# Stores of a PEER layer on ScalarE's queue, comparisons that read a PSUM bank, and pieces of the second layer's attention in other places

## The chip, the cores and the metric

The kernel runs on one core of a Trainium2 chip. The metric is device time in microseconds (us) of one execution. Five engines take part: PE (TensorE: matmuls; PEld are its weight loads), DVE (VectorE), ACT (ScalarE), POOL (GpSimd) and SP (SyncE, which issues DMAs). A DMA is issued by an instruction of an engine's queue; what stands behind that instruction waits until it is through.

## The reference, cut to what matters

A backbone of two layers over 512 latent and 256 context tokens, D = 1024, everything in float32. Each layer has an attention part and a PEER part (product-key experts with one neuron each).

```python
for l in range(2):
    sh1, s1, g1, sh2, s2, g2 = split(silu(c) @ w_mod[l] + b_mod[l])        # context: likewise from c_ctx
    hx = rms(x) * (1 + s1) + sh1
    q, k, v, u = split(hx @ w_in[l])
    q, k = rope(rms(q) * q_gain), rope(rms(k) * k_gain)
    o_attn = softmax(q @ [k_ctx, k].T) @ [v_ctx, v]
    o_conv = silu(layer_norm(depthwise_conv31(a * sigmoid(gate))))         # u = [a, gate]
    x = x + g1 * (concat(rms(o_attn) * beta_a, rms(o_conv) * beta_c) @ w_o[l])
    x = x + g2 * peer(rms(x) * (1 + s2) + sh2)
    if l == 0: h_ctx = ...                                                # the same for the context
return rms(x) * final_g

def peer(h):                          # 8 heads, 2 x 128 keys, 16384 experts
    s = (h @ w_pq) . sub_keys         # two scores lists of 128 for each head
    top 16 of each list, top 16 of the 16 x 16 sums -> expert (128 a token), w = softmax(best)
    return sum over experts of gelu(h . u_tab[expert]) * w * v_tab[expert]
```

In layer 1 the context is needed for its keys and values alone.

## The kernel before, in words

**Attention (`attention_layer`, L227 on).** Work is written as Python generators, and `merge` (L212) takes the next piece of the stream whose clock is furthest behind; the framework's scheduler then fixes each engine's order. Streams are the projections (`project`), the convolution taps (L406), modulations (`more_mods`, `mod`) and gathers of the PEER part before. Layer 1 loads `wqkv`, `convw`, `rope` and `gains` at its head (L283 to L286). `gq` (L289) is made of `gains`, `rot` (L293, L296) of `rope` and `gq`, and `hT` (L268 to L270) is the normalised x that the first product `qkv` (L319) reads. `context_kv` (L577) makes keys and values of one block of 128 context tokens: squares, a reciprocal root on DVE, a broadcast over the partitions (`rows`, L192), then `hC`, and the products; in layer 1 it is called once in `project` and once after the merge. `mod(l, s)` makes one of the six modulation vectors from four 1 MB blocks `wm` of the weights. The output projection (L683 on) opens two PSUM tiles with the convolution's half, `products(..., (4, 5, 6, 7))`, and then adds the attention's half, which reads `qs` (L485, L486).

**PEER (`peer_layer`, L707 on).** The latent tiles `dd` (four of 128 tokens in layer 0, td = 512; three in layer 1, td = 384) are computed densely over all 16384 experts; the other tiles (`fgt`) fetch their 128 experts a token with indirect DMAs on POOL (`uv`, L896), multiplied on DVE (L900: dot products, L889: weighted sums). The dense part runs in two stages.

- *U stage.* `u_stream` (L982) takes 128 steps. A step loads 512 KB of U (`raw`, two buffers, SP), splits it into `hi` (ACT, L989) and `lo` (POOL, L990), does 24 matmuls into a PSUM bank `ups` (L994; two banks in turn), takes the Gelu on ACT (`ge`, L996) and stores it to `gd` in DRAM (L998, issued by SP; the last 8 steps keep theirs).
- *Weights.* At the same time `w_stream` (L931) makes for each token the matrix of its expert weights over the 128 x 128 grid of keys: a one-hot comparison of the two key indices with the numbers 0 to 127 (`iota`, L955 on DVE, four tokens at a time, three buffers `o12`), scaled by the weight on ACT (L960), multiplied on PE (`wps`, L961), copied by ACT into `sg` (L963) and stored to `wd`, 2 MB for each block of 32 tokens (L965, issued by SP). The routing before it has a comparison of its own, `oh` (L813), in 100 x 8 numbers a partition.
- *V stage.* `v_stream` reads `gd` and `wd` back and multiplies with V (`vr`, L1024; `vps`, L1035).

The lines that decide the stores and the comparison:

```python
V.tensor_tensor(out=oh, in0=iota..., in1=c2[:, :, tt]..., op=ALU.is_equal)            # L955
nc.sync.dma_start(wd[:, :, (i - dd[0]) * 4 + blk]..., sg...)                          # L965
raw = up.tile([P, KD, P], F32, tag="raw", name="raw", bufs=2)                         # L985
nc.sync.dma_start(raw, io["uT"][l, c])                                                # L986
ps = pdd[0].tile([P, 512], F32, tag="dd", name="ups")                                 # L991
nc.sync.dma_start(gd[c // 4, :, c % 4], ge[:, 0:td])                                  # L998
```

Of the kernel before, what the change touches and what calls it, by code (L numbers as in the profile page):

```python
# [17 lines left out]
P = 128  # L18
# [26 lines left out]
T0 = (1.0, 1.0)  # L45
T1 = (2.0, 2.0)
CY = 2.0
# [13 lines left out]
def body(ctx: ExitStack, tc: tile.TileContext, io):  # L61
# [9 lines left out]
    def small(shape, name):  # L71
        pool, tag = cur["small"]
        return pool.tile(shape, F32, tag=tag, name=name)
# [153 lines left out]
    def attention_layer(l, st, fgs, fp, mark):  # L227
# [18 lines left out]
        work = pool("awk", 2, hst)  # L246
        hT = hp.tile([P, KD, nq * P], F32, tag="hT", name="hT")
        TW = SEQ if last else GW - 2 * PAD
        parts = [] if last else [(1, CT, [hT[:, k, SEQ:] for k in range(KD)])]
# [30 lines left out]
        convw = mid.tile([P, 4, CONVK], F32, name="convw")  # L280
        gains = hp.tile([P, 2, HD], F32, name="gains")

        wqkv = [wload(io["w_qkv"][l, c], "wqkv") for c in range(3)]  # L283
        nc.sync.dma_start(convw, io["convw"][:, l])
        nc.sync.dma_start(rope, io["rope"].rearrange("(n p) c d -> p n c d", p=P))
        nc.sync.dma_start(gains, io["gains"][l].partition_broadcast(P))  # L286

# [201 lines left out]
        def more_mods():  # L489
            for m in (((0, 2), (0, 3), (0, 4), (0, 5), (1, 0), (1, 1)) if l == 0 else ((1, 2), (1, 3), (1, 4), (1, 5))):  # L490
                yield from mod(*m, ppt)

        def conv_norm(t0, n, g0):
# [29 lines left out]
            for b in range(4):  # L523
                if t0:
                    V.scalar_tensor_tensor(yT[:, b, ys], yT[:, b, ys], vecs[:, l, b, 4:5], bc, op0=ALU.mult, op1=ALU.mult)
                else:
# [7 lines left out]
                    V.tensor_tensor(out=lo[:, 0:SEQ].rearrange("p (j t) -> p j t", j=hi.shape[1]), in0=q, in1=hi.bitcast(F32), op=ALU.subtract)  # L534
                    ylo.append(lo[:, 0:SEQ])
            done.append("latent" if t0 == 0 else "context")
            yield 2.0
# [39 lines left out]
        def context_kv(i):  # L577

            x = xT[:, :, i * P:(i + 1) * P]
            A.activation(hC, x, AF.Square)  # L580
            bc = rows(rsqrt(col_sums([hC[:, k, :] for k in range(KD)], 1), 1, 1.0 / D, EPS, "n"), 1)
            V.tensor_tensor(out=hC, in0=x, in1=bc.unsqueeze(1).to_broadcast([P, KD, P]), op=ALU.mult)
            V.tensor_tensor(out=hC, in0=hC, in1=mods[l, 1][:, :, 1:2].to_broadcast([P, KD, P]), op=ALU.mult)
            V.tensor_tensor(out=hC, in0=hC, in1=mods[l, 0][:, :, 1:2].to_broadcast([P, KD, P]), op=ALU.add)
            for _ in qkv(i):
                pass

        def project():
            for i in LAT if last else CT + LAT:
                yield from qkv(i)  # L590
                if last and i == LAT[-1]:
                    context_kv(NL)
            if last:
# [11 lines left out]
        if last:  # L605
            clock["mod"] = 100.0
            del streams["conv"]
            merge({**streams, "fg": (fgs, FD), "mod": (md, 2.4)}, clock, ("p", "fg"))
            with tc.high_priority():
                context_kv(NL + 1)  # L610
        else:
            merge(streams, clock, ("p",))
# [80 lines left out]
        for hf in range(4):  # L693
            if hf == len(ws):
                ws.append(wo_split(hf, op.tile([P, KD, WC], F32R, tag="whi", name="whi"), op.tile([P, KD, WC], F32R, tag="wlo", name="wlo")))
            while len(opened) < len(ws):
                opened.append(pbig.tile([P, 2, SEQ], F32, tag="big", name="wo"))
                products(opened[-1], ws[len(opened) - 1], (4, 5, 6, 7))
            ps = opened[hf]
            products(ps, ws[hf], (0, 1, 2, 3))  # L700
# [6 lines left out]
    def peer_layer(l, fp):  # L707
# [6 lines left out]
        with ExitStack() as outer:  # L714
# [16 lines left out]
            for i in dd:  # L731
                tops[i] = (rt.tile([P, PH, 2, TOPK], F32, name=f"top{i}"), rt.tile([P, PH, 2, TOPK], U32, name=f"tix{i}"))

            def best16(tiles, h, qT, keys, tmp):
# [50 lines left out]
            def route(i, rw, h0, h1):  # L785
# [25 lines left out]
                for h in range(h0, h1):  # L811
                    oh = rw.tile([P, TOPK, NCAND], F32, tag="oh", name="oh")
                    V.tensor_tensor(out=oh, in0=posf[:, h].unsqueeze(2).to_broadcast([P, TOPK, NCAND]),  # L813
                                    in1=iota[:, 0:NCAND].unsqueeze(1).to_broadcast([P, TOPK, NCAND]), op=ALU.is_equal)
                    (V if i == fgt[0] else G).tensor_tensor(out=oh, in0=oh, in1=cid[:, h].unsqueeze(1).to_broadcast([P, TOPK, NCAND]), op=ALU.mult)
# [115 lines left out]
            def w_stream():  # L931

                for i in dd:
# [16 lines left out]
                    for blk in range(4):  # L950
                        sg = rw.tile([P, PK // 2, 32, 2], F32, tag="sg", name="sg", bufs=2)
                        for t0 in range(0, 32, 4):
                            tt = slice(blk * 32 + t0, blk * 32 + t0 + 4)
                            oh = rw.tile([P, 2, 4, PK], F32, tag="o12", name="o12", bufs=3)
                            V.tensor_tensor(out=oh, in0=iota.unsqueeze(1).unsqueeze(1).to_broadcast([P, 2, 4, PK]), in1=c2[:, :, tt].to_broadcast([P, 2, 4, PK]), op=ALU.is_equal)  # L955
                            o1, o2 = oh[:, 0], oh[:, 1]
# [7 lines left out]
                            yield 1.9  # L964
                        nc.sync.dma_start(wd[:, :, (i - dd[0]) * 4 + blk].rearrange("g p h t e -> p g (h t e)"), sg.rearrange("p (g h) t e -> p g (h t e)", h=2))  # L965

# [15 lines left out]
            def u_stream():  # L982

                for c in range(PK):
# [5 lines left out]
                    mark.append(G.tensor_tensor(out=lo, in0=raw, in1=hi.bitcast(F32), op=ALU.subtract))  # L990
                    ps = pdd[0].tile([P, 512], F32, tag="dd", name="ups")  # L991
                    for n, (a, b) in enumerate(((hi, hhi), (hi, hlo), (lo, hhi))):
# [4 lines left out]
                    if c < PK - 8:  # L997
                        nc.sync.dma_start(gd[c // 4, :, c % 4], ge[:, 0:td])  # L998
                    else:
# [189 lines left out]
```

## Time and profile before

| | |
|---|---|
| three runs | 4172.8, 4183.14, 4179.64 us; median 4179.64 |
| the profiled execution | 4177.53 us, its span 4175.8 us |
| mean granted clock of PE | 0.953 of full speed |
| busy over the span | PE 90%, DVE 74%, ACT 43%, POOL 53% |
| attention of layer 0 | 0 to about 512 us |
| U stage of layer 0 | 512 to 1555 us |
| V stage of layer 0 | 1555 to 2316 us |
| attention of layer 1 | 2316 to 2738 us |
| U stage of layer 1 | 2738 to 3550 us |
| V stage of layer 1 and the end | 3550 to 4176 us |

A time in a row is counted from the start of the span. "[5.95 <-ACT hi L989]" behind an instruction says how long its engine had stood still before it, and which work ended last of what it waited for. An issue instruction of a DMA isn't counted as busy time.

### The profile page before, as it was taken

How to read it: one execution, taken by the hardware profiler on the slowest of the kernel's cores; microseconds unless marked ns; L12 is line 12 of the kernel's file. 1: busy time of each engine (PE TensorE's matmuls, PEld its weight loads, DVE VectorE, ACT ScalarE, POOL GpSimd, SP SyncE). 2: the span in 40 equal slices, each digit the busy share in tenths (PEclk: the TensorE clock that was granted, in tenths of full speed). 3: DMA queues.
4: the chain of work that ended last, by engine and by line, in shares of the span. 5: the costliest groups of instructions: out<-in, count | busy, mean ns of one | idle time of the engine just before them, and what ended most of it. 6: DMA issues, size and time to landing. Idle time of an engine off the chain costs nothing. (4 is left out here: it accounts for less than half of the span.)

```text
span 4175.8 us, 54192 instructions
## 1 busy us (share of the span) xinstructions
PE 3769.0 (90%) x19278; PEld 3204.7 (77%) x19278; DVE 3098.4 (74%) x5680; ACT 1811.6 (43%) x3679; POOL 2216.7 (53%) x1223
## 2 busy tenths in 40 slices
PE   8879998989988999999999779889888989898998
PEld 6547776867777777888777547679888888898897
DVE  5693369999986647898887784389877453787885
ACT  3345233336675633333333246333466564333333
POOL 0580135666665456555556356135756555665664
PEclk9989999999999999999999889899999999999999
DMA  4142135987888888988887714046676878898884
GB/s 169 58 182 81 51 119 204 331 304 244 285 285 287 268 319 338 344 322 335 339 335 292 275 41 172 21 136 241 231 247 220 259 262 283 320 345 297 315 319 140
DMA packets 327631, 1003.72 MB, mean 240 GB/s; under 512 B 24384, under 2 KB 159808, under 8 KB 264256
## 3 DMA queue, kind: packets, MB, share of 16 engines
q1 hardware_dynamic: 266128, 580.25, 40.5%
q0 software_dynamic: 59904, 419.46, 27.1%
q8 instruction: 152, 2.49, 0.2%
q14 instruction: 119, 0.97, 0.1%
q10 hardware_dynamic: 1328, 0.55, 0.0%
HBM read 884.29 MB, written 115.87 MB: 240 GB/s over the span
## 5 line engine op out<-in xcount | busy, mean ns | idle before, releaser
L990 POOL TENSOR_TENSOR lo<-raw,hi 128x1024 fp32r<-128x1024 f32 x256 | 647.1, 2529 | 572.0 <-ACT hi L989 504.7
L1028 POOL TENSOR_TENSOR vlo<-vr,vhi 128x1024 fp32r<-128x1024 f32 x256 | 629.5, 2466 | 471.4 <-ACT vhi L1027 457.4
L1035 PE MATMUL vps<-ahi,vhi 128*128 128x512 f32 (+1 forms) x2048 | 759.7, 372 | 44.5 <-DVE xT L1038 26.5
L1035 PE MATMUL vps<-alo,vhi 128*128 128x512 f32 (+1 forms) x2048 | 757.4, 370 | 3.1 <-DVE alo L974 3.1
L1035 PE MATMUL vps<-ahi,vlo 128*128 128x512 f32 (+1 forms) x2048 | 740.2, 371 | 9.2 <-POOL vlo L1028 9.1
L900 DVE SCALAR_TENSOR_TENSOR uv<-uv,hp 128x1024 f32<-128x1024 f32 x363 | 439.7, 1211 | 212.2 <-DMA uv<-in_uv,uix 212.1
L994 PE MATMUL ups<-hhi,hi 128*128 128x512 f32 (+1 forms) x2048 | 504.9, 386 | 72.2 <-ACT ge L996 34.7
L889 DVE SCALAR_TENSOR_TENSOR yp<-uv,act,yp 128x1024 f32<-128x1024 f32 x359 | 460.4, 1283 | 144.9 <-ACT act L902 144.0
L896 POOL DMA_INDIRECT uv<-in_uv,uix x384 | 447.8, 1166 | 222.0 <-DVE y L889 45.4
L994 PEld LDWEIGHTS ups<-hhi,hi 128*128 128x128 f32 x2048 | 383.7, 198 | 127.6 <-ACT ge L996 41.3
L994 PE MATMUL ups<-hhi,lo 128*128 128x512 f32 (+1 forms) x2048 | 479.0, 371 | 1.8 <-POOL lo L990 1.8
L994 PE MATMUL ups<-hlo,hi 128*128 128x512 f32 (+1 forms) x2048 | 475.1, 370 | 0.0
L1035 PEld LDWEIGHTS vps<-ahi,vhi 128*128 128x128 f32 x2048 | 391.3, 191 | 99.8 <-DVE xT L1038 30.6
L1035 PEld LDWEIGHTS vps<-ahi,vlo 128*128 128x128 f32 x2048 | 389.7, 191 | 63.2 <-POOL vlo L1028 16.2
L1035 PEld LDWEIGHTS vps<-alo,vhi 128*128 128x128 f32 x2048 | 391.6, 191 | 51.4 <-DVE alo L974 4.4
L901 ACT ACTIVATE act<-dots 128x1 f32<-128x1 f32 x384 | 77.4, 202 | 803.5 <-DVE uv L900 802.5
L994 PEld LDWEIGHTS ups<-hlo,hi 128*128 128x128 f32 x2048 | 378.8, 192 | 40.5
L994 PEld LDWEIGHTS ups<-hhi,lo 128*128 128x128 f32 x2048 | 373.4, 191 | 40.6 <-POOL lo L990 2.4
L955 DVE TENSOR_TENSOR o<-iota,xf 128x1024 f32<-128x1024 f32 x224 | 385.9, 1749 | 21.0 <-ACT o L960 9.3
L410 POOL TENSOR_TENSOR yT<-yT,tp 128x512 f32<-128x512 f32 (+1 forms) x150 | 261.4, 1743 | 211.9 <-ACT tp L409 201.7
L989 ACT CAST hi<-raw 128x1024 fp32r<-128x1024 f32 x256 | 267.0, 1043 | 217.8 <-DMA raw<-in_uT 185.3
L960 ACT ACTIVATE o<-o,wT 128x128 f32<-128x128 f32 x896 | 285.1, 392 | 152.2 <-DVE o L955 150.7
(281 smaller groups left out, 6055.0 us busy)
## 6 DMA issues: line engine op xcount, KB each, us to landing
raw<-in_uT SPq DMA_DIRECT2D x256, 512.0 KB, 4.9
vr<-in_vq SPq DMA_DIRECT2D x256, 512.0 KB, 6.0
wd<-sg SPq DMA_DIRECT2D x28, 2048.0 KB, 13.5
wm<-in_w_mod SPq DMA_DIRECT2D x48, 1024.0 KB, 6.5
w<-wd SPq DMA_DIRECT2D x32, 1024.0 KB, 6.6
gd<-ge SPq DMA_DIRECT2D x120, 256.0 KB, 6.2
ge<-gd SPq DMA_DIRECT2D x60, 512.0 KB, 7.1
w<-wd SPq DMA_DIRECT2D x32, 768.0 KB, 6.2
```

The source lines that it names most:

```text
L410: G.tensor_tensor(out=y, in0=y, in1=tp, op=ALU.add)
L889: V.scalar_tensor_tensor(y, t[:, 1, :], act[:, e:e + 1], y, op0=ALU.mult, op1=ALU.add)
L896: got = G.indirect_dma_start(out=t.rearrange("p c d -> p (c d)"), out_offset=None, in_=io["uv"], in_offset=bass.IndirectOffsetOnAxis(ap=ui ...
L900: V.scalar_tensor_tensor(t[:, 0, :], t[:, 0, :], 1.0, at["h"], op0=ALU.mult, op1=ALU.mult, accum_out=dots[:, ec])
L901: A.activation(act[:, ec], dots[:, ec], AF.Gelu)
L955: V.tensor_tensor(out=oh, in0=iota.unsqueeze(1).unsqueeze(1).to_broadcast([P, 2, 4, PK]), in1=c2[:, :, tt].to_broadcast([P, 2, 4, PK]), op ...
L960: A.activation(o2[:, j, :], o2[:, j, :], AF.Copy, scale=wT[:, t:t + 1])
L989: A.copy(hi, raw)
L990: mark.append(G.tensor_tensor(out=lo, in0=raw, in1=hi.bitcast(F32), op=ALU.subtract))
L994: PE.matmul(ps[:, 0:td], a[:, k, :], b[:, k, :], start=k == 0 and n == 0, stop=k == KD - 1 and n == 2)
L1028: mark.append(G.tensor_tensor(out=vlo, in0=raw, in1=vhi.bitcast(F32), op=ALU.subtract))
L1035: PE.matmul(ps[:, 0:td], a[:, c % 4, d * P:(d + 1) * P], b, start=c == 0 and n == 0, stop=c == 7 and n == 2)
```

## The change

1. The stores of `wd` and `gd` are issued by ACT (`nc.scalar`) in place of SP, in both layers.
2. In layer 1, where td + 128 = 512, a copy of `iota` is put into columns 384 to 511 of one of the two `ups` banks; both banks are then fixed tiles (`dds`), used in turn by even and odd steps, and both comparisons (L955, L813; now L982, L840) read the copy.
3. `gains` gets its place in a pool of the whole kernel, and its load stands at the start of `attention_layer`; the load of `rope` stands ahead of `wqkv` in the code.
4. `mod(1, 5)` leaves layer 1's modulation stream and stands in the output projection, between the opening products and those that read `qs`.
5. `context_kv` is a generator with pauses; its second call is a stream `k` of its own that starts when the gathers and the first call are done.
6. In layer 1 `conv_norm` pauses after each block; a pace of layer 0's taps goes from 2.0 to 2.6.

```diff
-T1 = (2.0, 2.0)
+T1 = (2.6, 2.0)
...
+        gains = sm.tile([P, 2, HD], F32, tag="dg", name="gains")
+        nc.sync.dma_start(gains, io["gains"][l].partition_broadcast(P))
...
-        gains = hp.tile([P, 2, HD], F32, name="gains")
+        nc.sync.dma_start(rope, io["rope"].rearrange("(n p) c d -> p n c d", p=P))
         wqkv = [wload(io["w_qkv"][l, c], "wqkv") for c in range(3)]
         nc.sync.dma_start(convw, io["convw"][:, l])
-        nc.sync.dma_start(rope, io["rope"].rearrange("(n p) c d -> p n c d", p=P))
-        nc.sync.dma_start(gains, io["gains"][l].partition_broadcast(P))
...
-            for m in (((0, 2), (0, 3), (0, 4), (0, 5), (1, 0), (1, 1)) if l == 0 else ((1, 2), (1, 3), (1, 4), (1, 5))):
+            for m in (((0, 2), (0, 3), (0, 4), (0, 5), (1, 0), (1, 1)) if l == 0 else ((1, 2), (1, 3), (1, 4))):
...
+                    if last:
+                        yield 4.5
...
-            bc = rows(rsqrt(col_sums([hC[:, k, :] for k in range(KD)], 1), 1, 1.0 / D, EPS, "n"), 1)
+            ps = small([P, P], "cs4")
+            spread(ps, [(ones[:, 0:32], hC[:, k, :]) for k in range(KD)], P)
+            yield 3.0
+            r = rsqrt(fold(ps, 1), 1, 1.0 / D, EPS, "n")
+            yield 8.0
+            bc = rows(r, 1)
...
-            for _ in qkv(i):
-                pass
+            yield 5.0
+            yield from qkv(i)
+            done.append(i)
...
-                    context_kv(NL)
+                    yield from context_kv(NL)
...
-            merge({**streams, "fg": (fgs, FD), "mod": (md, 2.4)}, clock, ("p", "fg"))
-            with tc.high_priority():
-                context_kv(NL + 1)
+            def gathered():
+                yield from fgs
+                done.append("fg")
+            def late_context():
+                while not {"fg", NL}.issubset(done):
+                    yield 1.0
+                yield from context_kv(NL + 1)
+            merge({**streams, "fg": (gathered(), FD), "mod": (md, 2.4), "k": (late_context(), 1.0)}, clock, ("p", "k"))
...
+            if last and not hf:
+                for _ in mod(1, 5, ppt):
+                    pass
             ps = opened[hf]
...
+            dds, num = [], iota
+            if td + PK <= 512:
+                dds = [pdd[0].tile([P, 512], F32, tag=f"dd{j}", name="ups", bufs=1) for j in range(2)]
+                num = dds[0][:, td:td + PK]
+                V.tensor_copy(num, iota)
...
-                                    in1=iota[:, 0:NCAND].unsqueeze(1).to_broadcast([P, TOPK, NCAND]), op=ALU.is_equal)
+                                    in1=num[:, 0:NCAND].unsqueeze(1).to_broadcast([P, TOPK, NCAND]), op=ALU.is_equal)
...
-                            V.tensor_tensor(out=oh, in0=iota.unsqueeze(1).unsqueeze(1).to_broadcast([P, 2, 4, PK]), in1=c2[:, :, tt].to_broadcast([P, 2, 4, PK]), op=ALU.is_equal)
+                            V.tensor_tensor(out=oh, in0=num.unsqueeze(1).unsqueeze(1).to_broadcast([P, 2, 4, PK]), in1=c2[:, :, tt].to_broadcast([P, 2, 4, PK]), op=ALU.is_equal)
...
-                        nc.sync.dma_start(wd[:, :, (i - dd[0]) * 4 + blk].rearrange("g p h t e -> p g (h t e)"), sg.rearrange("p (g h) t e -> p g (h t e)", h=2))
+                        nc.scalar.dma_start(wd[:, :, (i - dd[0]) * 4 + blk].rearrange("g p h t e -> p g (h t e)"), sg.rearrange("p (g h) t e -> p g (h t e)", h=2))
...
-                    ps = pdd[0].tile([P, 512], F32, tag="dd", name="ups")
+                    ps = dds[c % 2] if dds else pdd[0].tile([P, 512], F32, tag="dd", name="ups")
...
-                        nc.sync.dma_start(gd[c // 4, :, c % 4], ge[:, 0:td])
+                        nc.scalar.dma_start(gd[c // 4, :, c % 4], ge[:, 0:td])
```

What the built programs issue, at the places of the prediction (line numbers of the changed kernel are larger by 2 to 27). SP before, around the last `wd` store of layer 1:

```order
L986 DMA raw<-in_uT 128x1024
L998 DMA gd_20098<-ge 128x384
L965 DMA wd_20099<-sg 128x32x128
L986 DMA raw<-in_uT 128x1024
L998 DMA gd_20098<-ge 128x384
```

ACT of the changed kernel, around one `wd` store of layer 1 (L990 is the copy into `sg`, L1016 the cast to `hi`, L1023 the Gelu, L928 and L929 belong to the gathers):

```order
L1016 CAST hi<-raw 128x1024
L990 COPY sg<-wps 128x4x64x2
L1023 ACTIVATE ge<-ups 128x384 x2
L992 DMA wd_20099<-sg 128x32x128
L1025 DMA gd_20098<-ge 128x384 x2
L928 ACTIVATE act<-dots 128x1
L929 ACTIVATE act<-act,wk 128x1
L1016 CAST hi<-raw 128x1024
```

The next store stands directly behind `wd`, now on ACT, with a cast of `hi` behind both; on SP the loads of `raw` follow each other with no store between.

DVE of the changed kernel in layer 1's U stage, with what each instruction waits for (Activation is ACT, DMASW the gathers' DMAs):

```order
L982 TENSOR_TENSOR o_22474<-ups,xf 128x1024 [waits DVE_49,Activation_49]
L982 TENSOR_TENSOR o_22486<-ups,xf 128x1024 [waits DVE_49,PE_49]
L982 TENSOR_TENSOR o_22539<-ups,xf 128x1024 [waits DVE_49,PE_49]
L927 SCALAR_TENSOR_TENSOR uv,dots<-uv,hp 128x1024 [waits DMASW1_49]
L916 SCALAR_TENSOR_TENSOR yp<-uv,act,yp 128x1024 [waits DVE_49,Activation_49]
L982 TENSOR_TENSOR o_22584<-ups,xf 128x1024 [waits DVE_49,Activation_49]
```

And PE of the changed kernel there, at an even step, an odd one and the next even one:

```order
L1021 MATMUL ups<-hhi,hi 128x384 [waits DVE_49]
...
L1021 MATMUL ups<-hhi,hi 128x384 [waits Activation_49]
L1021 MATMUL ups<-hhi,hi 128x384 x7
L1021 MATMUL ups<-hlo,hi 128x384 x8
L1021 MATMUL ups<-hhi,lo 128x384 [waits Pool_49]
L1021 MATMUL ups<-hhi,lo 128x384 x7
L988 MATMUL wps<-o_23886 128x128 [waits PE_49,Activation_49]
L988 MATMUL wps<-o_23886 128x128 [waits Activation_49] x2
L1021 MATMUL ups<-hhi,hi 128x384 [waits DVE_49]
```

The first comparison of a group waits for ACT, by the program for the Gelu of the even step, and 48 of the even steps begin with a wait for DVE; before, no step's first matmul had that wait.

DVE at the head of layer 1, before:

```order
L196 TENSOR_TENSOR dg<-ident,rs_y 128x512
L289 TENSOR_SCALAR gq<-gains 128x64
L290 COPY gq<-gains 128x64
L268 TENSOR_TENSOR hT<-xT,rbc 128x8x128
L204 TENSOR_TENSOR hT<-xT,rbc 128x384 x8
L293 TENSOR_TENSOR rot<-rope,gq 128x4x64
L296 TENSOR_TENSOR rot<-rope,gq 128x4x32 x2
```

and changed:

```order
L289 TENSOR_SCALAR gq<-gains 128x64
...
L196 TENSOR_TENSOR dg<-ident,rs_y 128x512
L293 TENSOR_TENSOR rot<-rope,gq 128x4x64
L296 TENSOR_TENSOR rot<-rope,gq 128x4x32 x2
L270 TENSOR_TENSOR hT<-xT,rbc 128x8x128
L204 TENSOR_TENSOR hT<-xT,rbc 128x384 x8
```

`gq` moved ahead of the reciprocal root, and `rot` ahead of `hT`; SP loads `rope` behind `wqkv` and `convw` as before.

## Rows read from the trace of the kernel before

**Rows 1.** Busy time by stage: us, then PE, PEld, DVE, ACT, POOL, clock, DMA, GB/s.

```profile
512.00:1555.00 1043.00, 946.78 (x4490) 779.93 (x4490) 864.10 (x2025) 529.03 (x1240) 582.76 (x316) 0.96 0.78 262
...
2316.00:2738.00 422.00, 337.86 (x1768) 239.90 (x1766) 245.80 (x466) 178.37 (x300) 172.62 (x116) 0.88 0.32 116
2738.00:3550.00 812.00, 723.55 (x4222) 705.83 (x4223) 581.99 (x1323) 418.19 (x949) 472.17 (x238) 0.95 0.72 239
```

**Rows 2.** The chain that ended last, 2740 to 3550 us, shares by line.

```profile
by line: PE ups L994 20.3%; DMA raw<-in_uT 15.6%; DMA uv<-in_uv,uix 8.6%; DVE o L955 5.7%; PE wps L961 5.1%; issue 4.2%; DVE oh L813 3.5%; POOL lo L990 3.4%; DVE uv L900 3.2%; DVE yp L889 3.1%; DVE eid L816 2.3%; DVE tix L746 1.8%; DVE sc L
```

**Rows 3.** Waits of PE, 2738 to 3550: total us, times, longest.

```profile
PE wps L961 <- ACT sg L963: 31.0, 14, 5.6
```

**Rows 4.** The page's groups: count, busy us, mean ns, idle before.

```profile
L989 ACT CAST hi<-raw 128x1024 fp32r<-128x1024 f32 x256 | 267.0, 1043 | 217.8 <-DMA raw<-in_uT 185.3
```

**Rows 5.** Timeline around one wd store (start, duration us): SP, ACT, PE.

```profile
3278.24 0.37 SPq L965 DMA_DIRECT2D wd<-sg  x1
3278.72 8.58 SPq L986 DMA_DIRECT2D raw<-in_uT  x1
...
3292.39 1.04 ACT L989 CAST hi<-raw 128x1024 fp32r<-128x1024 f32 x1 [7.97 <-DMA raw<-in_uT]
...
3293.48 2.93 PE L994 MATMUL ups<-hhi,hi 128*128 128x384 f32 x8 [5.95 <-ACT hi L989]
```

**Rows 6.** Line 986: duration of the issue, ns min/median/max.

```profile
L986 SPq DMA_DIRECT2D raw<-in_uT x256: 327/333/11621, 508.5 to 3539.0; - x128
```

**Rows 7.** Timeline: first and last held issue, first and last PE gap.

```profile
985.79 5.04 SPq L998 DMA_DIRECT2D gd<-ge  x1
...
3460.82 8.11 SPq L986 DMA_DIRECT2D raw<-in_uT  x1
...
998.26 0.67 PE L961 MATMUL wps<-o 128*128 128x128 f32 x3 [1.37 <-ACT o L960]
...
3474.41 1.97 PE L994 MATMUL ups<-hhi,hi 128*128 128x384 f32 x5 [5.38 <-ACT hi L989]
```

**Rows 8.** The page's DMA queues: packets, MB, share of 16 engines.

```profile
q10 hardware_dynamic: 1328, 0.55, 0.0%
```

**Rows 9.** Timeline at layer 1's head: SP, DVE, PE; last the landings.

```profile
2318.53 0.44 SPq L285 DMA_DIRECT2D rope<-in_rope  x1
...
2338.70 0.20 DVE L289 TENSOR_SCALAR gq<-gains 128x64 f32<-128x64 f32 x1 [13.30 <-DMA gains<-in_gains]
...
2347.75 4.63 PE L319 MATMUL qkv<-wqkv,hT 128*128 128x256 f32 x13 [18.73 <-DVE rs_y L148]
...
rope<-in_rope SPq DMA_DIRECT2D x2, 256.0 KB, 12.1
```

**Rows 10.** Timeline of PE in layer 1's attention.

```profile
2463.66 0.80 PE L197 MATMUL rows<-dg,ones 128*128 128x128 f32 x2 [8.59 <-DVE dg L196]
```

**Rows 11.** PE at the output projection, and the modulations' busy time, 2316 to 2738.

```profile
2689.85 8.47 PE L689 MATMUL wo<-qs,w 128*128 128x512 f32 x24 [5.99 <-DVE qs L486]
...
2316.00:2738.00 422.00, 21.45 (x256) 8.52 (x256) 4.68 (x8) 0.88 0.32 116
```

**Rows 12.** Lines 955 and 900: ns min/median/max; then the mean in layer 1.

```profile
L955 DVE TENSOR_TENSOR o<-iota,xf x96: 1209/1221/5220, 3004.9 to 3444.5; 128x1024 f32<-128x1024 f32 x96
...
L900 DVE SCALAR_TENSOR_TENSOR uv<-uv,hp x363: 1187/1210/1225, 684.0 to 4091.8; 128x1024 f32<-128x1024 f32 x182
...
L955 DVE TENSOR_TENSOR o<-iota,xf 128x1024 f32<-128x1024 f32 x96 | 166.0, 1761 | 14.3 <-ACT o L960 8.0 <-PE wps L961 4.8 <-ACT ge L996 1.4
```

**Rows 13.** Layer 1's U stage: one step, one wps, the Gelu, DVE's longest wait.

```profile
3235.83 4.17 PE ups L994 x24
...
3273.77 1.05 PE L961 MATMUL wps<-o 128*128 128x128 f32 x8
...
L996 ACT ACTIVATE ge<-ups 128x384 f32<-128x384 f32 x127 | 61.1, 481 | 31.6 <-DMA gd<-ge 19.1 <-PE ups L994 12.5
...
DVE uv L900 <- DMA uv<-in_uv,uix: 131.0, 33, 10.3
```

## The prediction

> **What bounds the kernel now.** I began with the table of the stages that the change touches [rows 1]. TensorE (PE) is the busiest engine in each, so the change can only pay where PE stands still: 96 us in the dense U stage of layer 0 (1043 - 947), 84 us in the attention of layer 1 at a clock of 0.88, and 88 us in the dense U stage of layer 1. The chain of waits over the last [rows 2] is not PE alone: the load of raw has 15.6% of it (127 us of 810), the one-hot comparison L955 5.7% and L813 3.5%. PE's waits there [rows 3] give the next link: the largest ends on ACT, at the copy sg. ACT's own wait stands behind it: hi waits 185.3 us for raw over both layers [rows 4].
>
> Why raw is late is seen at one store of wd [rows 5]. SP issues wd at 3278.24; its next instruction, the issue of raw, then takes 8.58 us instead of 0.33, until 3287.30. Raw lands 13.59 us after 3278.72, ACT casts at 3292.39, and PE resumes at 3293.48 after 5.95 us of nothing. The median of a raw issue is 0.33 us and the maximum 11.6 [rows 6]. 27 of the 28 wd stores are followed by such a hold of the next gd or raw issue, the first 5.04 and the last 8.11 us [rows 7], 160.6 us together.
>
> **The profiled execution** took 4177.53 us, 2.1 below the median of 4179.64; the sum is made against 4177.5.
>
> **wd and gd go from SP to ACT's queue.** What it can give: the 26 PE gaps over 0.7 us that end 3 to 20 us after a wd store, from 1.37 us before 998 to 5.38 us before 3474 [rows 7], add up to 25 us in layer 0 and 44 us in layer 1, so 69 us is the upper end. SP's holds don't vanish, since the changed order puts a gd directly behind wd on ACT: if ACT is held there to the moment SP was, hi starts at 3287.3 instead of 3292.4, because raw has landed meanwhile, and 4 to 5 of the 5.95 us are won. If in the other extreme each hold stops PE in full, 160.6 us come in place of the 69, a loss of 92. I take a gain of 30, under half of the upper end: by the built order ACT casts hi more than a step ahead, and a step of 24 matmuls covers 4.17 us [rows 13] of a hold of 6 on average. Against it stand 268 issues on ACT, taken at the 0.33 us of raw and the 0.37 of wd [rows 5, 6]: 88 us of ACT's time. ACT is busy 51% of both U stages [rows 1], and PE waits there for it; with a tenth of that exposed (bounds 0 and 88) it is +8. Net: **-22**.
>
> Beside the queue that carries SP's loads the trace lists a second hardware queue with 0.55 MB [rows 8], which fits the three small issues that ACT has before (512, 20 and 4 KB). Whether a hold on one also holds the other, no row shows. The Trainium skill (DMA: Bandwidth & Descriptors, Issuing engines are not separate DMA queues) says that issuing from several engines saves only sequencer time, usually a small part of the transfer. Here that time itself is large, a hold of 8.58 us before a landing of about 5. By the page's rule alone the term would be 0 or a few us.
>
> **gains leaves the head of layer 1.** Before, DVE waits 13.30 us for gains, and PE 18.73 us behind it [rows 9]. Now gains lies there already, but the changed order puts the rot products that read rope ahead of hT. Rope was issued at 2318.53, ahead of gains; the landing known of it, that of layer 0, took 12.1 us. So it lands between 2330.6 and the 2338.7 at which DVE went on: 0 to 8 us are won, and the rot products are only moved. I take **-4**.
>
> **context_kv in pieces.** PE waits 8.59 us for dg, whose reciprocal root stands between convolution taps on DVE [rows 10]. Now the second block comes late, in a stream of its own, and its chain is split. Its work isn't less and taps go on beside it: 0 to 8.6 us, and I take **-6**, nearer to the upper end because the wait is that of the chain that is split. The pause in conv_norm and the new pace of layer 0 move only order; in layer 0 DVE's order before the U stage is the same, so nothing is taken for them.
>
> **mod(1,5) goes into the output projection.** PE waits 5.99 us there for qs, and the four modulations of layer 1 cost PE 21.45 us, one 5.4 [rows 11]. Placed in the gap it saves that at most; if its weights come late or qs is no longer late, 0. I take **-4**.
>
> **The comparisons read PSUM.** L955 has a median of 1221 ns, a maximum of 5220 and, in layer 1, a mean of 1761: 96 x 0.54 = 52 us of stretching. DVE's L900, of the same size and with an operand in PSUM, never leaves 1187 to 1225 in 363 instructions [rows 12]. So I expect about 1.22 us each, and the like of L813. Only what is on the chain pays: 46 us of L955 and 28 of L813 [rows 2], of which the stretched share of 30% (0.54 of 1.76) is 22; with the next delay close behind I take **-12** (0 to -22).
>
> **The bank becomes shared.** The built order shows what it costs: a group of L982 waits for the Gelu of the even step, and the next even step's first matmul waits for DVE, 48 times. Per pair PE has 2 x 4.17 us and three wps groups of 1.05 [rows 13], 11.5 in all; the new cycle is an even step of 4.17, a Gelu of 0.48 [rows 13], three comparisons of 1.22 and one or two gather products of 1.21: 9.5 to 10.7. It just fits. It doesn't where a gather product waits for its rows in between. DVE waits for uv 131 us in 33 pieces there [rows 13], 4 us each. I take **+8**; bounds 0 and, with 20 of those pieces exposed, +80.
>
> **Sum:** -22 - 4 - 6 - 4 - 12 + 8 = -40, so 4177.5 - 40 = **4137.5 us**.
>
> **The rivals.**
>
> *ACT is held and PE with it (slower).* One place: the gd behind wd on ACT, in the 16 + 12 blocks. For it: PE waits on ACT [rows 3], and a held ACT does no cast, no Gelu and no scaling, where a held SP stopped only the next load. Against: ACT's 49% of idle time. The point where it decides: the other terms give -18 and the issues +8, so -10, and the removed gaps 69; above 79 us of exposed holds, half of the 160.6, the kernel is slower. With 110 exposed it is 4177.5 - 10 - 69 + 110 = 4208.5.
>
> *The bank ties DVE to PE (slower).* With the upper bound of 80 in place of 8: -40 + 72 = +32, so 4209.5. It decides from 40 us of exposed gather waits above the 8 on. For it: DVE is busy 72% of that stage [rows 1] and waits for gathers; against: the cycle of 9.5 to 10.7 fits under 11.5.
>
> *The stores hold SP from ACT's queue too.* Then raw is as late as before, the 30 us fall away, and the sum is 4167.5; with some holds on ACT as well up to 4180. For it: a gd was held just like raw [rows 7], so the hold follows from wd and not from the held transfer. Against it: the second queue [rows 8]. By the Trainium skill (Perfetto Trace Analysis, DMA Instruction, on hardware-generated descriptors) the generator is shared and locked for one instruction at a time, and a profile's issue time includes the wait for that lock; by it this case is the expected one. No run here shows it yet.
>
> *More than I count.* If nearly all of the 69 us go and the stretching as well, -69 + 8 - 8 - 8.6 - 5.4 - 22 + 8 = -97: about 4080.
>
> **How the numbers follow.** The forecast has 0.48, the common generator 0.16, held ACT 0.16, the bank 0.10, more than counted 0.10. The range should hold eight in ten: from 4085, nearly the large gain, to 4205, just under the two slow cases. A measurement can tell about 0.3% (12.5 us) from no change. Faster: nearly all of the forecast (0.44), the large gain and a quarter of the common generator, 0.58. Same: most of that rival, a little of the forecast and of held ACT, 0.18. Slower: the slow cases, 0.24. If it is faster, I expect 4085 to 4165.
>
> **What would show it.** Right: raw issues of 0.33 us throughout; ACT hi waiting under 100 us for raw instead of 185; held gd issues of 4 to 8 us on ACT, with PE gaps after them under 2 us; L982 with mean near 1.22 us; the U stages together 30 to 50 us shorter; PE's gap at the head of layer 1 some 14 us. Wrong: PE gaps of 5 us behind wd on ACT (held ACT), raw still held (common generator), or PE waiting for DVE at even steps for more than 30 us (the bank).

## The result, and the profile after

The changed kernel takes 4296.37 us (median of four runs), the kernel before 4181.39 beside it: a ratio of 1.0282, 95% interval 1.0259 to 1.0305. It is 115 us slower, where the prediction said 40 us faster. The time lies above the range, 4085 to 4205 us.

The spans of the profiled executions are 4294.3 and 4175.8 us. Cut at PE's first instruction of each kind (first ups, first wps, first and last vps of layer 0, first qkv, ups, wps and vps of layer 1), both traces give:

```
stage (us)                              before   after   difference
attention, layer 0                       525.9   547.9     +22.0
U stage, layer 0, ahead of the weights   425.5   424.3      -1.2
U stage, layer 0, with the weights       631.4   656.1     +24.7
V stage, layer 0                         733.1   731.1      -2.0
head of layer 1 (last vps to first qkv)   31.8    31.7      -0.1
attention, layer 1                       391.4   380.1     -11.3
U stage, layer 1, ahead of the weights   268.3   257.5     -10.8
U stage, layer 1, with the weights       554.2   669.7    +115.5
V stage, layer 1, and the end            614.1   595.9     -18.2
```

The two parts of layer 1's U stage belong together, since the weights begin after fewer steps than before (ahead of them PE runs 1090 matmuls in place of 1356): 822.5 us before, 927.2 after, +105. The busy times of that stage, before and after (columns as in [rows 1]):

```profile
2739.00:3562.00 823.00, 727.98 (x4239) 709.93 (x4240) 588.81 (x1331) 421.19 (x958) 474.05 (x240) 0.95 0.72 240
```

```profile
2771.00:3698.00 927.00, 747.38 (x4238) 718.93 (x4238) 516.00 (x1331) 428.31 (x957) 433.38 (x239) 0.93 0.63 212
```

The work is the same (the counts agree). DVE is busy 73 us less, as the faster comparisons should give. But PE idles 180 us instead of 95, and at a granted clock of 0.93 in place of 0.95 the same matmuls take 19 us more. The waits of PE and DVE there, after (total us, times, longest):

```profile
PE ups L1021 <- ACT ge L1023: 56.9, 45, 2.8
PE ups L1021 <- DVE oh L840: 53.9, 12, 16.8
PE wps L988 <- ACT o L987: 31.9, 8, 6.5
...
PE ups L1021 <- DVE o L982: 4.7, 2, 4.3
...
PE wps L988 <- ACT sg L990: 1.5, 2, 1.3
...
DVE uv L927 <- DMA uv<-in_uv,uix: 172.4, 46, 11.4
DVE o L982 <- ACT ge L1023: 71.2, 21, 7.2
...
DVE eid L843 <- POOL oh L842: 48.9, 14, 7.4
...
DVE oh L840 <- ACT ge L1023: 20.1, 8, 5.1
```

Before, PE's largest wait in this stage was the copy sg [rows 3], now 1.5 us; it waited 16.2 us for Gelus and for no comparison. Now it waits 56.9 us for Gelus and 58.6 us for comparisons, 53.9 of it for the routing comparison L840 in only 12 pieces. DVE's largest wait is still the one for the gathered rows, 172.4 us where it was 131.8; its 91 us for Gelus (71.2 + 20.1) are new, 1.4 us before. The longest PE wait for a comparison, on the timelines of PE, ACT and DVE (start, duration):

```profile
2948.83 1.55 PE L1021 MATMUL ups<-hhi,lo 128*128 128x384 f32 x8
2967.15 2.29 PE L1021 MATMUL ups<-hhi,hi 128*128 128x384 f32 x6 [16.77 <-DVE oh L840]
...
2945.38 0.49 ACT L1023 ACTIVATE ge<-ups 128x384 f32<-128x384 f32 x1 [1.46 <-DMA gd<-ge]
...
2958.50 0.97 DVE L840 TENSOR_TENSOR oh<-posf,ups 128x800 f32<-128x800 f32 x1
...
2966.13 0.97 DVE L840 TENSOR_TENSOR oh<-posf,ups 128x800 f32<-128x800 f32 x1
```

The bank's Gelu was through at 2945.9, and the bank free for the next even step. But in the program's order two routing comparisons come first, and DVE reaches the first only after some 85 small routing instructions and two gather products, the second after some 35 more and two more products. The second ends at 2967.10, and 0.05 us later PE goes on. Before, PE did not depend on that chain until the weights needed it.

The stores went as intended on SP's side. The issue of raw, whose maximum was 11.6 us [rows 6], and ACT's first held issue after:

```profile
L1013 SPq DMA_DIRECT2D raw<-in_uT x256: 327/328/469, 530.2 to 3676.9; - x128
...
1005.60 0.39 ACTq L992 DMA_DIRECT2D wd<-sg  x1
1006.03 9.65 ACTq L1025 DMA_DIRECT2D gd<-ge  x1
```

Raw is never held again. 20 raw issues fall into stretches in which ACT's queue is held, and each takes 0.33 us: a hold on ACT's queue does not reach SP's. ACT's hi waits 50.3 us for raw in the whole execution, where it waited 185.3 [rows 4]. But the hold came along with wd. Of gd and raw issues over 1.5 us the trace before has 30 on SP, 165.8 us in sum; the one after 26 on ACT, 156.8 us. No cast, scaling or copy starts on ACT later than 1.3 us into a hold. In layer 0's U stage with the weights, 24.7 us longer, PE waits for just these pieces, the copy sg and the scaling o:

```profile
PE wps L988 <- ACT sg L990: 32.2, 14, 6.2
PE wps L988 <- ACT o L987: 27.4, 16, 7.4
```

Before, the two were 19.7 and 17.7 us there. The PE gaps over 0.7 us within 20 us after a wd store sum to 47.8 us in layer 0, where they were 25.4.

The one-hot comparison lost its stretching (columns as in [rows 12]), and the stage is longer all the same:

```profile
L982 DVE TENSOR_TENSOR o<-ups,xf x96: 1198/1215/1227, 3027.0 to 3594.5; 128x1024 f32<-128x1024 f32 x96
```

At the head of layer 1, gains is there early, and rope has taken its place (timeline of DVE and PE, to be read beside [rows 9]):

```profile
2382.09 0.43 DVE L293 TENSOR_TENSOR rot<-rope,gq 128x256 f32<-128x256 f32 x1 [12.77 <-DMA rope<-in_rope]
...
2391.11 1.22 PE L319 MATMUL qkv<-wqkv,hT 128*128 128x256 f32 x2 [18.17 <-DVE rs_y L149]
```

### The profile page after: what moved, and what is told of

Read it like the earlier page. It is cut to its first block, busy times and chain, and to the rows that moved or that the text cites. A ratio compares the mean times of both kernels' runs of the same rounds, so it can differ in the third digit from the quotient of the medians.

```text
span 4294.3 us, 54046 instructions
## 1 busy us (share of the span) xinstructions
PE 3794.1 (88%) x19278; PEld 3213.0 (75%) x19278; DVE 2994.1 (70%) x5681; ACT 1808.9 (42%) x3672; POOL 2177.9 (51%) x1223
## 4 chain that ended last, share of the span: by engine, by line
PE 38%; DVE 10%; DMA 9%; issue 4%; ACT 3%; POOL 3%; ACTq 2%; SPq 0%; POOLq 0%; DVEq 0%
PE vps L1062 22%; PE ups L1021 8%; DMA uv<-in_uv,uix 4%; PE wps L988 2%; ACTq L1025 1%; DMA raw<-in_uT 1%; DMA vr<-in_vq 1%; DVE alo L1001 1%; POOL vlo L1055 1%; DVE ge L997 1%; DVE uv L927 1%; ACT ge L1023 1%; PE po L460 1%; PE wo L705 1%; DVE yT L406 1%
## 5 line engine op out<-in xcount | busy, mean ns | idle before, releaser
L1017 POOL TENSOR_TENSOR lo<-raw,hi 128x1024 fp32r<-128x1024 f32 x256 | 631.6, 2468 | 768.8 <-ACT hi L1016 550.9
L1021 PE MATMUL ups<-hhi,hi 128*128 128x512 f32 (+1 forms) x2048 | 518.2, 393 | 170.5 <-ACT ge L1023 68.2
L923 POOL DMA_INDIRECT uv<-in_uv,uix x384 | 429.3, 1118 | 211.6 <-DVE y L916 42.7
L928 ACT ACTIVATE act<-dots 128x1 f32<-128x1 f32 x384 | 77.3, 201 | 811.8 <-DVE uv L927 781.9
L1016 ACT CAST hi<-raw 128x1024 fp32r<-128x1024 f32 x256 | 266.7, 1042 | 237.8 <-PE ups L1021 163.6
L988 PE MATMUL wps<-o 128*128 128x128 f32 x1792 | 259.0, 289 | 93.4 <-ACT o L987 59.4
```

Source lines behind the costliest of these rows:

```text
L923: got = G.indirect_dma_start(out=t.rearrange("p c d -> p (c d)"), out_offset=None, in_=io["uv"], in_offset=bass.IndirectOffsetOnAxis(ap=ui ...
L928: A.activation(act[:, ec], dots[:, ec], AF.Gelu)
L988: PE.matmul(ps[:, j, :], o1[:, j, :], o2[:, j, :], start=True, stop=True)
L1016: A.copy(hi, raw)
L1021: PE.matmul(ps[:, 0:td], a[:, k, :], b[:, k, :], start=k == 0 and n == 0, stop=k == KD - 1 and n == 2)
```

## The experiments

The theory after the result: the shared bank makes layer 1's U stage longer, and the stores and T1 account for layer 0. Its rival: ACT, held behind wd, does it in both layers. In the table "U1" is layer 1's U stage from the first ups to the first vps, "U0w" layer 0's U stage with the weights, "att0" and "att1" the attentions, "V1" layer 1's V stage with the end; profiled executions, us. The same stage of the same order differs by up to 9 us from one profile to another, and a profile isn't always of a typical execution: that of best is its slowest of 12 (4196.23 us), those of stores_only and T1_only are their fastest of 6.

```
run             att0    U0w    head   att1    U1      V1     ratio to before (95%)
before          525.9   631.4  31.8   391.4   822.5   614.1  1
after           547.9   656.1  31.7   380.1   927.2   595.9  1.0282 (1.0259 to 1.0305)
stores_only     527.6   636.8  32.1   393.7   819.6   622.9  1.0052 (1.0026 to 1.0077)
stores_back     544.4   623.0  31.6   379.8   929.8   607.5  1.0246 (1.0210 to 1.0281)
attention_only  548.7   626.4  31.8   382.6   818.5   613.4  1.0012 (0.9996 to 1.0028)
T1_only         550.5   633.7  32.0   387.6   817.5   617.5  1.0076 (1.0052 to 1.0100)
fixed_banks     546.5   623.2  31.7   386.7   827.0   621.8  one run, 4198.80 us
half_bank       545.2   625.3  31.6   380.2   904.5   609.0  one run, 4258.54 us
eq_only         547.4   627.4  31.8   381.3   873.3   591.7  one run, 4220.59 us
oh_only         539.4   639.0  31.4   383.7   883.5   623.1  1.0144 (1.0117 to 1.0171)
rot_late        532.7   641.6  19.6   381.9   886.0   620.0  1.0123 (1.0094 to 1.0152)
best            541.0   636.6  19.6   387.6   825.6   627.0  0.9983 (0.9971 to 0.9995)
split_only      533.4   617.1  32.1   389.8   808.2   618.1  0.9941 (0.9919 to 0.9963)
best_split      532.2   621.2  19.6   384.7   801.9   623.6  0.9915 (0.9894 to 0.9936)
```

**stores_only**: the kernel before, with both stores on ACT.

```diff
-                        nc.sync.dma_start(wd[...
+                        nc.scalar.dma_start(wd[...
-                        nc.sync.dma_start(gd[...
+                        nc.scalar.dma_start(gd[...
```

> Only the two stores are moved to ACT; the bank, the attention and T1 are those of before. Theory bank (the shared PSUM bank makes layer 1's weight stage 114 us longer, the stores cost about 24 us in layer 0 and 10 to 20 in layer 1): 4215 to 4225 us, ratio 1.008 to 1.011, layer 1's weight stage at most 20 us longer. Rival stores (ACT, held at the store behind wd, makes that loss too): 4285 to 4300 us, ratio about 1.027, layer 1's weight stage 90 to 114 us longer.

Measured: 4204.95 us, layer 1's weight stage 549.9 against 554.2. The rival falls. The stores cost 0.5%, a little less than the theory's 0.8 to 1.1%; no one stage of the profile holds that loss. Why they gain nothing is in the trace: hi waits 100.0 us for raw in place of 185.3, but the holds moved as they were (26 on ACT, 141.0 us), and the PE gaps over 0.7 us within 20 us after a wd store changed from 25.4 to 37.0 us in layer 0 and from 42.8 to 27.8 in layer 1: 68 before, 65 now. One such hold on ACT, and the raw issues:

```profile
3254.88 0.47 ACT L996 ACTIVATE ge<-ups 128x384 f32<-128x384 f32 x1
3255.39 6.28 ACTq L998 DMA_DIRECT2D gd<-ge  x1
...
L986 SPq DMA_DIRECT2D raw<-in_uT x256: 327/328/727, 510.5 to 3544.1; - x128
```

**stores_back**: the changed kernel with the stores on SP.

> The changed kernel with both stores issued by SP again; the bank, the attention and T1 stay changed. Theory bank: layer 1's weight stage stays 80 to 100 us longer than before, the time is 4250 to 4265 us, ratio 1.017 to 1.021. Rival stores: the stage is as short as before and the time 4185 to 4200 us, ratio 1.001 to 1.005.

Measured: 4279.42 us, U1 929.8. The loss in layer 1 stays in full without the stores, and was not smaller but larger than I expected of the bank: the weight stage is 117.5 us longer where I said 80 to 100, and the total is above the 4250 to 4265. Against this run the changed kernel, which differs in the stores alone, has 33 us more in U0w and about the same U1.

**attention_only**: the same without the bank.

```diff
-            if td + PK <= 512:
+            if False:
```

> The changed kernel with the stores back on SP and without the bank: what is left is T1, gains and rope, mod(1,5), context_kv and conv_norm. Both theories: layer 0's attention 22 us longer, layer 1's 11 us shorter, the U stages as before, so 4188 to 4196 us, ratio about 1.002 to 1.004. If these edits also shift the dense stages, the time would be over 4210.

Measured: 4186.6 us, a little under the expected time, the stages as expected. With stores_back it isolates the bank: 929.8 - 818.5 = 111 us of U1, but 92.8 us of the whole (4279.42 - 4186.6), since V1 is 6 us shorter with the bank and other stages differ by a few us. By the medians the changes so far add up: nothing that can be told from 0 for the attention edits with T1, 93 us for the bank, 17 for the stores beside them (4296.37 - 4279.42, from two comparisons whose intervals overlap), 111 of the 115 us.

**T1_only**: the kernel before with `T1 = (2.6, 2.0)`.

> The kernel before with the one pace T1 of layer 0 at 2.6. Theory pace (the later taps and not gains or rope make layer 0's attention longer): 4200 to 4206 us, ratio 1.004 to 1.006. Rival (the early load of gains delays x, and the rest follows): as before, 4178 to 4184 us, ratio 0.999 to 1.001.

Measured: 4211.55 us, ratio 1.0076, more than expected; layer 0's attention 550.5. So the pace does lengthen it. About half of the 24.6 us is one chain at the end of the convolution, and not the taps: DVE's first 453 instructions are the same as before, to about 395 us, all 61 taps among them. The reciprocal root of the last layer norm, at 394.9 us before, among the attention's products, comes at 441.4. The norm behind it moves along with it, to where PE has nothing else to do: PE stands 11.8 us, until 480.7. PE's waits between 300 and 552 us for such a chain, before and in T1_only:

```profile
PE rows L197 <- DVE dg L196: 6.1, 2, 5.3
...
PE rows L197 <- DVE dg L196: 18.0, 3, 11.8
```

The wait is 17.9 or 18.0 us in each of the seven profiles with 2.6, and 6.1 or 6.2 in each of the seven with 2.0. Over all profiles the attention of layer 0 takes 544 to 551 us in the seven with 2.6 and 526 to 541 in the seven with 2.0, 14 us apart on average. In the runs that also have the other attention edits part of it comes back in U0w (623 to 627 against 637 to 642), so what T1 costs the whole is settled only for this run alone.

**fixed_banks**: as stores_back, but both comparisons read `iota`.

```diff
-                                    in1=num[:, 0:NCAND]...
+                                    in1=iota[:, 0:NCAND]...
-                            V.tensor_tensor(out=oh, in0=num...
+                            V.tensor_tensor(out=oh, in0=iota...
```

> As stores_back, with the two fixed ups banks, but both comparisons read iota in SBUF again; the copy stays unread. Theory sharing (the reading of a bank that PE fills is what costs): layer 1's weight stage falls from 672 back to 545 to 560 us, total 4180 to 4195. Rival rotation (fixed tiles in place of the pool's rotation cost it): the stage stays above 650 us, total about 4280.

Measured: U1 827.0, its weight stage 556.8; the total, of one run, is 4 us above the expected 4180 to 4195. It is the reading, not the fixed pair of banks. By the reading is meant all that follows from it in the program: the built order changes with it too (ahead of the first weights PE runs 1356 matmuls here as before, 1090 in every run whose one-hot comparisons read the bank, 1134 where the routing alone does). No run has that order without the readers.

**half_bank**: L982 reads the bank in two of four blocks.

```diff
+                            ... in0=(num if blk < 2 else iota)...
```

> As stores_back, but of the four blocks of 32 tokens of each tile only the first two read the PSUM copy in L982, the last two read iota in SBUF; the routing comparison reads PSUM. Theory sharing: half of the 117 us go, the weight stage of layer 1 takes 600 to 625 us and the steps of the last two blocks are as short as before (about 6.3 us a step), those of the first two about 8. Rival (the loss comes from the order of the whole stage, which the scheduler sets around the bank): the stage is above 645 us or below 575.

Measured: the weight stage 649.5, above the 600 to 625 of the theory and, by its number, where the rival put it (above 645); U1 904.5. Half of L982's readers give back 25 us of the 103 between stores_back and fixed_banks. Either the order of the whole stage counts or the other reader does, the routing comparison; this run can't tell which.

**oh_only**: T1 at 2.0, stores on SP; only the routing comparison L840 reads the bank.

```diff
-T1 = (2.6, 2.0)
+T1 = (2.0, 2.0)
-                            V.tensor_tensor(out=oh, in0=num...
+                            V.tensor_tensor(out=oh, in0=iota...
```

> Stores on SP, T1 back at 2.0, all other attention edits kept; only the routing comparison L840 reads the PSUM copy, the one-hot comparison L982 reads iota in SBUF. Expected by the stages so far: layer 0's attention as before, layer 1's attention 9 to 12 us shorter, the part of layer 1's U stage ahead of the weights about 10 us shorter, the weight stage as before: 4155 to 4168 us, ratio 0.994 to 0.997. Rival (any reader of the shared bank delays the U steps): the weight stage over 580 us and the total over 4190.

Measured: 4250.81 us, ratio 1.0144. My expectation failed and its rival held: 32 reading instructions make U1 61 us longer than before. PE's largest wait of that stage is for them:

```profile
PE ups L1021 <- DVE oh L840: 50.3, 10, 17.3
```

**eq_only**: as stores_back; only L982 reads the bank.

> As stores_back (T1 2.6, stores on SP), but only the 96 one-hot comparisons L982 read the PSUM copy; the 32 routing comparisons L840 read iota in SBUF. Theory two readers: each of the two readers of the bank costs by itself; layer 1's U stage from its first step to the first V product takes about 870 us against 822 before, 930 with both and 884 with the routing alone, and PE waits for L840 nowhere. Rival (the routing comparison alone costs, the one-hot comparisons ride on it): 822 to 835 us.

Measured: U1 873.3 us, the 870 expected; PE waits for L840 nowhere. Against fixed_banks (827.0) the 96 one-hot comparisons cost 46 us of U1; the 32 routing comparisons cost 58 to 60 (oh_only or rot_late less best, below; rot_late differs from best in that reading alone). Together 104 to 106, and stores_back has 103 (929.8 - 827.0): about 0.5 us for each one-hot comparison and 1.8 for each in the routing. The 46 are not spread evenly: PE waits once there, for 18.3 us, for the routing's sum eid, which it does for 1.2 us in the changed kernel. And they are not all lost: V1 is 30 us shorter here than in fixed_banks, and the spans differ by 22 us only (4218.8 and 4197.0, one run each). The routing's 60 stay: rot_late's V1 is 7 us below best's, and its median is 58 us above.

**rot_late**: as oh_only, with `rot` ordered behind `hT` in layer 1.

```diff
+            if last:
+                for m in made:          # the rot products of this qk
+                    tc.add_manual_dep(m.ins, first.ins.name, ..., reason="late")   # first: the last hT of the first block
```

> As oh_only, and in layer 1 the four rot products, which read rope, are ordered behind hT. Theory head (hT waited only for whatever small load stood ahead of it on DVE, first gains, then rope): the 31.8 us from the last V product to the first qkv product fall to 18 to 23, the total is 8 to 13 us below oh_only, 4143 to 4160, ratio 0.991 to 0.995. Rival (wqkv itself is late, or the wait turns up at the next user of rot): the head or the attention behind it keeps its length and the total is that of oh_only within 4 us.

Measured: the head falls from 31.4 to 19.6 us, the median by 12.0, as the theory said of the difference; the time itself, 4238.82, is not the 4143 to 4160, which started from oh_only as I had expected it. The intervals of the two ratios overlap; the head shows it clearly. hT had only ever waited for what stood ahead of it in DVE's order.

**best**: rot_late without the bank.

> T1 at 2.0, stores on SP, no reader of the shared bank, the attention edits and rot behind hT: the parts of the change that shortened a stage, and the mended head. Expected: layer 0's attention 526 to 533 us, the head 19.6 in place of 31.8, layer 1's attention 382 in place of 391, the U and V stages as before: 4158 to 4168 us, ratio 0.993 to 0.997. Rival (layer 0's attention is longer by the early gains and not by T1): 4170 to 4180.

Measured: 4180.52 us, ratio 0.9983, barely faster than before: my expectation failed, and the time lies at the upper end of the rival's. The head (-12) and layer 1's attention (-4) are there; layer 0's attention was 541.0 in that profile, longer than the 526 to 533 expected. The four profiles with T1 at 2.0 and the other attention edits have 532 to 541, the three without those edits 526 to 533, so something beside T1 may lengthen it too; 7 us on average, within what one profile differs from another, settle nothing.

**best_split**: as best, and each wd store in two halves on two queues.

```diff
-                        nc.sync.dma_start(wd[..., blk]..., sg...)
+                        to, fr = wd[..., blk]..., sg...
+                        half = PK // 8
+                        nc.scalar.dma_start(to[:, 0:half], fr[:, 0:half])
+                        nc.sync.dma_start(to[:, half:], fr[:, half:])
```

> As best, and each 2 MB store of wd is split: one half issued by ACT, one by SP. Theory capacity (the issue behind wd is held because one queue takes in so much at a time): each queue's half holds its next issue much less, under 2 us in place of 6, the PE gaps within 20 us after a store fall from 68 to under 30 us, and the time is 20 to 40 us below best. Rival (the store's bytes hold everything whatever the queue): holds of 4 us and more on SP and ACT both, time as best or above.

Measured: 4150.0 us, ratio 0.9915, faster than both kernels and 30 us below best, inside the 20 to 40 expected. The held issues over 1.5 us fall to 20 on SP, 63.9 us in sum (19 and 62.0 of them raw and gd), a mean of 3.2 us and not under 2. ACT has none, but it issues nothing else within 20 us of its half, so its queue could show none. The PE gaps after the stores fall to 51 us, not under 30.

**split_only**: the kernel before with that one edit.

> The kernel before with the one edit that each wd store is split, half issued by ACT and half by SP. Theory capacity: the holds behind wd on SP fall from 166 us to about 60 and none is on ACT, the two weight stages together are 25 to 35 us shorter, 4150 to 4160 us, ratio 0.992 to 0.995. Rival (the gain of best_split over best was another order of the stages, or chance): 4178 to 4188, ratio 0.998 to 1.001.

Measured: 4159.44 us, ratio 0.9941, as expected, and the two weight stages together are 30 us shorter, as expected; the holds, 24 on SP, still sum to 82.1 us where I said 60. The split carries most of best_split's gain by itself. By what it gains is less clear: the PE gaps after the stores are 62 us here, only 6 below before, and hi still waits 168.4 us for raw.

## Why the prediction was wrong, point by point

- **The bank, the step that failed.** It stood in the sum as +8, with 80 as its upper bound; it measures +103 to +111 in the stage and 93 in the whole kernel. Two things went wrong. I worked out the cycle of a pair of steps for the one-hot comparisons only: they cost 46 us of the stage where I took 8. And I let the routing comparison in as a gain alone ("the like of L813"), though the order gives every reader of the copy the same place between two even steps. The 32 routing comparisons cost 58 to 60 us: DVE comes to them through a long chain of small instructions with gather products between, and PE's 16.77 us above is one of 12 such waits. The rival "the bank ties DVE to PE" was the right mechanism; it had a chance of 0.10 and its price was read from gather waits alone. Its sign, PE waiting for DVE over 30 us, came true with 58.6.
- **The comparisons read PSUM.** Right in the size of an instruction (1.215 against 1.22 us) and in DVE's busy time; wrong as a term (-12). fixed_banks and attention_only, with the stretched comparison, have the shorter U stage; no run has the quick comparison without the shared bank, so what it would be worth alone isn't shown.
- **The stores, -22.** Measured +20 alone (4204.95 against 4185.31) and +17 beside the other changes. Taking wd off SP did free raw, as I said. The 30 us of gain failed: I looked at hi alone, of which ACT casts more than a step ahead, but a held ACT also makes no copy sg and no scaling o, and PE waits for those. The gaps after the stores stayed at 65 us in stores_only, where they were 68, 0.5% to the bad. In the changed kernel layer 0's gaps are 47.8 us where stores_back has 23.2, and its weight stage is 33 us longer; there the rival "ACT is held and PE with it" describes what happens. Why the same move costs that stage 33 us here and 5 in stores_only stays open. The rival in which the stores hold SP from ACT's queue too is refuted: raw's longest issue is 0.469 us. That speaks against what I drew from the Trainium skill (Perfetto Trace Analysis, DMA Instruction), a lock that both queues share as long as a hold lasts. The Trainium skill's other place cited (DMA: Bandwidth & Descriptors, Issuing engines are not separate DMA queues), by which I put the term at about 0, came out nearer than my estimate.
- **T1, taken at nothing.** I wrote that DVE's order in layer 0 before the U stage was the same. In T1_only it is the same to about 395 us; behind that the last norms of the convolution come later, PE waits 18.0 us for them in place of 6.1, and that attention is 24.6 us longer. What is left of it in the whole of the changed kernel isn't settled.
- **gains, -4.** Measured 0. The step looked for rope's landing in one earlier load (12.1 us); here it took 20.2 (issued at 2361.86, used at 2382.09), the last in its queue as gains had been. rot_late shows that the wait was one of order: -12.
- **context_kv and mod(1,5), -10.** Layer 1's attention is 11.3 us shorter, and 9 to 12 in stores_back and attention_only; on average the ten profiles with these edits are 8 us below the four without. Right in size; the two parts, and conv_norm's pause, were not separated.
- **Unforeseen and open:** layer 1's V stage is 18 us shorter after. The table shows what it goes with: V1 is 592 to 609 us in the four runs whose one-hot comparisons read the bank, and 613 to 627 in the ten others, so part of what the bank costs in the U stage comes back here. The same 61 gathers are left at its start, and PE waits 8.4 us for DVE's xT in place of 21.5; the cause stays open.

## What to carry to other kernels

Before operands are put into the spare columns of a buffer that another engine keeps refilling, list every reader and, for each, what stands ahead of it on its engine: each becomes a condition for the next refill. Here an instruction that is stretched on an engine off the critical path was cheaper than one that is fast and tied. Where a store holds the queue behind it, moving it moved the hold here, so ask what else the other engine does for PE; splitting the store over two queues shortened the hold. Compare whole times too, and not only the stage that a change is meant for: with the one-hot comparisons alone on the bank that stage was 46 us longer and the next one 30 us shorter.

## What the runs showed of the hardware that was not expected

A 2 MB store issued whole holds the next issue of its own queue on either engine (mean 5.5 us on SP over 30 issues before, 5.4 on ACT over 26 in stores_only), and an issue on the other queue not at all (raw at most 0.727 us). Halved between both queues the holds of raw and gd sum to 62 to 82 us in place of 166. They are all on SP, which issues raw and gd; ACT issues nothing within 20 us behind its half, so whether a half would hold ACT's queue isn't shown.
